# Late rms factor in the fronts, another order in the attention to the memory, and C and D normalised on ScalarE

## The chip, the cores and the metric

The kernel runs on one core of a Trainium2 chip. A core has TensorE (PE in the profile), VectorE (DVE), ScalarE (ACT), GpSimd (POOL) and SyncE (SP), which issues the transfers. Each engine takes its instructions in the order in which the built program lists them and waits at an instruction until its semaphores allow it. The metric is the device time of one execution in microseconds, lower is better.

## The reference

Two layers of an encoder over 512 tokens of width 1024, in float32, with 256 memory tokens. A layer has three residual sub-layers: a mixer with four parallel attention branches A, B, C and D, each projected, gated and summed; an attention to the memory with four heads; and a squared-ReLU MLP. Every softmax attention scales its queries and keys by an rms norm per head, and that is what the change touches:

```
def rms(x, g):
    y = xf * lax.rsqrt(jnp.mean(xf * xf, axis=-1, keepdims=True) + EPS)
    return (y * g.astype(F32)).astype(x.dtype)
...
q = axial_rope(rms(q, g_qk[0]), row, col)
k = axial_rope(rms(k, g_qk[1]), row, col)
sc = jnp.einsum('bqgrd,bkgd->bgrqk', qg, k).astype(F32) * scale
p = jax.nn.softmax(sc, axis=-1)
```

The rms factor is one number per token and head. The gain works per channel, and the rotation mixes two channels of the same head, so the factor may be multiplied in before or after both.

## The kernel before

Matrix products run in a split form: an operand is a high part (rounded to the matmul's float32r) and a low part (the remainder), and `mm3` (L176) issues three matmuls, high by high, high by low and low by high, at L177 to L179. Weights come from DRAM into `wst` (3 buffers), ACT casts them to `whi` (L299, 4 buffers) and POOL subtracts to get `wlo` (L167 with POOL, four pieces for each tile).

The mixer of a layer is a list of units: four of B (a pair of heads each), four of A (one head), two of C and two of D (a group of four heads). A unit has a *front* and an *attention*. A front projects four blocks of 128 tokens (`tok_proj`, L386), evacuates each block from PSUM to `tok` and sums the squares per head into `sf` (`evac_sq`, L406 to L416), and then works in halves of two blocks each (`half`): the rms factor by `rpow` (L309: POOL adds, then POOL raises to the power -0.5), the factor times q and k on DVE (L452 in A, L552 in C and D, L722 in B), the gain (L454, L555, L557, L725), the rotation in B and D (`rope`, L576, at L584 to L587), the split into `spl` (ACT casts the high part, DVE subtracts for the low part, shown at L167 with DVE), and PE transposes of `spl` (`trans`, L399, shown at L403 in PE). The attention of a unit runs over 128 queries at a time: scores into an `sc` bank, maximum on DVE, exponentials on ACT with their sum (L634 in C, L638 in D), reciprocal of the sum (L640) and the product with it on DVE (L641), transposes on PE (L476), the split of the transposed `pt` (L479 on ACT, L480 on DVE), and the product with v.

Between the units stand pieces of the gates and branch projections, given by the string `FILL` (L90), chained in order of issue, so that PE has work while a front or an attention waits. The order of the whole program on each engine is set when it is built, by a scheduler that works from the order of issue, the buffers and its own estimate of durations.

The attention to the memory (`xattn`, L899) projects the queries of all four blocks first (`proj`, L907; PSUM tag `dn` with 2 banks), norms and splits each block (`xnorm_split`, L884), transposes them (`q_trans`, L910), and attends for two pairs of blocks and two pairs of heads (`attend`, L917), then projects out (L962). PSUM has 2 banks for `dn`, 2 for `sc`, 2 for `tr`, 1 for `pv` and 1 for `df`.

Of the kernel before, what the change touches and what calls it, by code (L numbers as in the profile page):

```python
# [93 lines left out]
def kernel(  # L94
# [41 lines left out]
    def ptile():  # L136
        return tl("p", [P, S + 2])
# [4 lines left out]
    def stat(n):  # L142
        return tl("st", [P, 8])[:, :n]
# [287 lines left out]
    def front_A(l, norm, h):  # L431
# [15 lines left out]
        def half(j):  # L447
# [85 lines left out]
    def front_G(l, norm, br, g):  # L533
# [14 lines left out]
        def half(j):  # L548
            tk, s = toks[j], st[j]
            rpow(s, s, 64 * EPS, 10)  # L550
            qk = tk[:, :, :320].rearrange("p t (h d) -> p t h d", h=5)
            V.tensor_tensor(out=qk, in0=qk, in1=bc(s.rearrange("p (t h) -> p t h", t=2), 3, 64), op=ALU.mult)  # L552
# [23 lines left out]
    def rope(x, tab, j, nh, nax):  # L576
# [3 lines left out]
        tmp = tl("zr", [P, S])[:, :2 * nh * w].rearrange("p (t h d) -> p t h d", t=2, h=nh)  # L580
# [22 lines left out]
    def attn_G(l, u, br, g, oslots):  # L603
# [5 lines left out]
        for j in range(4):  # L609
# [6 lines left out]
            for pr in range(2):  # L616
# [3 lines left out]
                for qi in range(2):  # L620
# [20 lines left out]
                    V.tensor_scalar(e, e, st[:, 2:3], None, op0=ALU.mult)  # L641
# [50 lines left out]
    def front_B(l, cT, p):  # L692
# [20 lines left out]
        for j in range(2):  # L713
            tk, s = toks[j]
            s3 = s.rearrange("p (t c) -> p t c", t=2)
            G.tensor_scalar(s3[:, :, 0:4], s3[:, :, 0:4], 64 * EPS, None, op0=ALU.add)
            G.tensor_scalar(s3[:, :, 4:6], s3[:, :, 4:6], 32 * EPS, None, op0=ALU.add)
            G.tensor_tensor(out=s, in0=s, in1=mhalf[:, :12], op=ALU.pow)
# [3 lines left out]
            V.tensor_tensor(out=qk, in0=qk, in1=bc(s3[:, :, 0:4], 3, 64), op=ALU.mult)  # L722
            V.tensor_tensor(out=qr, in0=qr, in1=bc(s3[:, :, 4:6], 3, 32), op=ALU.mult)
# [4 lines left out]
            rope(qr, bt_, j, 2, 1)  # L728
            sq_ = tl("spl", [P, 2, 2, 2, 96], F32R)
# [90 lines left out]
    def mem_prep(l):  # L820
# [3 lines left out]
        for c in range(2):  # L824
            st = tl("wst", [P, 4, NM])
            SY.dma_start(st, memT[c * 512:(c + 1) * 512, :].rearrange("(k p) t -> p k t", p=P))
            for k in range(4):
# [8 lines left out]
                else:  # L836
                    q = tl("zr", [P, S])[:, :NM]
# [61 lines left out]
    def xattn(l, norm, KT, VX, X, nm):  # L899
# [7 lines left out]
        def proj(pr):  # L907
            tok_proj(norm, views, S, ev, tbs=(2 * pr, 2 * pr + 1))
# [8 lines left out]
        def attend(pr):  # L917
            for hp in range(2):
                if hp == 1 and pr == 0:
                    q_trans(1)  # L920
                pth = tl("pt", [P, 2, 2, 256], F32R)
                ptl = tl("pt", [P, 2, 2, 256], F32R)
                for qi in range(2):
                    Tq = Tqs[2 * pr + qi]
                    ps = psum("sc").rearrange("p (h k) -> p h k", h=2)
                    for i in range(2):
                        h = 2 * hp + i
                        hs = slice(h * P, (h + 1) * P)
                        mm3(ps[:, i], Tq[:, 0, hs], Tq[:, 1, hs], KT[0][:, h, :], KT[1][:, h, :], True, True)
                    st = stat(6)  # L930
                    V.tensor_reduce(out=st[:, 0:2], in_=ps, axis=AX.X, op=ALU.max, negate=True)
                    e = ptile()[:, :S].rearrange("p (h k) -> p h k", h=2)
                    for i in range(2):
                        A.activation(e[:, i], ps[:, i], AF.Exp, bias=st[:, i:i + 1], accum_out=st[:, 2 + i:3 + i])
                    V.reciprocal(st[:, 4:6], st[:, 2:4])
                    V.tensor_tensor(out=e, in0=e, in1=bc(st[:, 4:6], 2, NM), op=ALU.mult)
                    qs = slice(qi * P, qi * P + P)
                    pt = psum("tr")
                    for i in range(2):
                        for kb in range(2):  # L940
                            T.transpose(pt[:, (2 * i + kb) * P:(2 * i + kb + 1) * P], e[:, i, kb * P:(kb + 1) * P], idf)
                    pv_ = pt.rearrange("p (k q) -> p k q", k=4)
                    hi = pth[:, :, :, qs].rearrange("p h k q -> p (h k) q")
                    lo = ptl[:, :, :, qs].rearrange("p h k q -> p (h k) q")
                    A.copy(hi, pv_)
                    V.tensor_tensor(out=lo, in0=pv_, in1=f(hi), op=ALU.subtract)
                po = psum("pv").rearrange("p (h q) -> p h q", h=2)
                for i in range(2):
                    h = 2 * hp + i
                    for kb in range(2):  # L950
                        hs = slice(h * P, (h + 1) * P)
                        mm3(po[:, i], VX[0][:, kb, hs], VX[1][:, kb, hs], pth[:, i, kb, :], ptl[:, i, kb, :], kb == 0,
                            kb == 1)
                for i in range(2):
# [321 lines left out]
```

## Time and profile before

| | |
|---|---|
| median of 3 runs | 2363.65 us (2363.37 to 2367.36) |
| profiled execution | 2361.96 us |
| its span, first to last instruction | 2360.0 us |
| PE busy | 2281.5 us, 97% of the span |
| DVE, ACT, POOL busy | 1384.1, 1151.8, 1299.0 us |
| mean granted PE clock | 0.992 of full speed |
| chain that ended last | PE 83%, DVE 11%, POOL 2% |

A time on the device holds the span and about 2 us around it. PE's busy time is the time in which at least one matmul is under way; matmuls overlap each other, so that two of them start 0.23 us apart while each is shown with 0.39 us. An idle stretch of PE is printed in brackets behind the instruction that ended it, with the instruction that released it. The granted clock is 1.00 at 2.4 GHz and 0.50 at 1.2 GHz. The layers lie at 20 to 1206 us and 1206 to 2360 us; in the first, B takes about 20 to 225 us, A to 430, C to 537, D to 690, the last branch work and the output projection to 764, the attention to the memory to 850, and the MLP the rest.

### The profile page before, as it was taken

What the parts mean: (1) busy time and instruction counts of PE and PEld (TensorE: products, weight loads), DVE (VectorE), ACT (ScalarE), POOL (GpSimd) and SP (SyncE); (2) the same over time, 40 slices, a digit from 0 to 9 for tenths busy, and PEclk for the clock granted to TensorE, in tenths of its full rate; (3) what the DMA queues carried; (4) which work ended last, traced back from release to release, by engine and by line L of the source; (5) the groups of instructions that cost most, each with busy time, mean ns of one, the idle gap of its engine ahead of it and who ended that gap; (6) DMA issues with size and microseconds to landing.
All of it is one profiled execution on the core that took longest, in us unless ns stands there. A gap on an engine that the chain in (4) does not pass through costs nothing.

```text
span 2360.0 us, 33643 instructions
## 1 busy us (share of the span) xinstructions
PE 2281.5 (97%) x12032; PEld 1966.0 (83%) x12032; DVE 1384.1 (59%) x2980; ACT 1151.8 (49%) x2253; POOL 1299.0 (55%) x1657
## 2 busy tenths in 40 slices
PE   8999999998999899999999998999989999999999
PEld 7888889887888888888888887898878878888887
DVE  7778666888975642222457786568879648222222
ACT  4556556655653543223345565566556546322321
POOL 7553544625465376666665435355353754766663
PEclk9999999999999999999999999999999999999999
DMA  5321342442454133333343214324425531323332
GB/s 185 108 94 57 102 138 66 127 154 84 147 179 155 54 99 98 98 92 96 111 134 101 83 46 127 113 79 134 136 92 168 171 131 56 106 91 97 98 93 77
DMA packets 88775, 258.25 MB, mean 109 GB/s; under 512 B 9704, under 2 KB 12392, under 8 KB 88608
## 3 DMA queue, kind: packets, MB, share of 16 engines
q1 hardware_dynamic: 88608, 256.10, 34.4%
q8 instruction: 95, 1.56, 0.3%
q14 instruction: 72, 0.59, 0.1%
HBM read 222.46 MB, written 33.60 MB: 109 GB/s over the span
## 4 chain that ended last, share of the span: by engine, by line
PE 83%; DVE 11%; POOL 2%; issue 1%; ACT 1%; DMA 1%; SPq 0%; POOLq 0%; ACTq 0%; DVEq 0%
PE dn L177 13%; PE dn L178 13%; PE dn L179 13%; PE df L177 10%; PE df L179 9%; PE df L178 9%; PE tr L476 3%; PE sc L177 1%; PE sc L179 1%; PE sc L178 1%; PE dn L403 1%; POOL wlo L167 1%; DVE pt L480 1%; DVE zr L584 1%; PE sc L624 1%
## 5 line engine op out<-in xcount | busy, mean ns | idle before, releaser
L167 POOL TENSOR_TENSOR wlo<-wst,whi 128x256 fp32r<-128x256 f32 (+3 forms) x1400 | 1071.0, 797 | 745.4 <-ACT whi L299 671.3
L299 ACT CAST whi<-wst 128x1024 fp32r<-128x1024 f32 (+3 forms) x350 | 348.8, 1003 | 640.8 <-PE dn L178 293.7
L177 PE MATMUL df<-s,whi 128*128 128x512 f32 (+1 forms) x967 | 381.0, 394 | 8.1 <-DVE zg L785 3.2
L179 PE MATMUL df<-s,wlo 128*128 128x512 f32 (+1 forms) x967 | 376.1, 389 | 1.3 <-POOL wlo L167 1.3
L178 PE MATMUL df<-s,whi 128*128 128x512 f32 (+1 forms) x967 | 374.3, 387 | 1.6 <-DVE s L167 1.6
L177 PE MATMUL dn<-whi,s 128*128 128x384 f32 (+4 forms) x768 | 264.8, 348 | 13.6 <-ACT s L348 7.7
L179 PE MATMUL dn<-whi,s 128*128 128x384 f32 (+4 forms) x768 | 263.3, 343 | 0.0
L178 PE MATMUL dn<-wlo,s 128*128 128x384 f32 (+4 forms) x768 | 263.1, 344 | 0.0
L177 PEld LDWEIGHTS df<-s,whi 128*128 128x128 f32 x967 | 181.7, 188 | 46.6 <-DVE yl L808 6.1
L179 PEld LDWEIGHTS df<-s,wlo 128*128 128x128 f32 x967 | 181.8, 188 | 38.4 <-POOL wlo L167 2.9
L178 PEld LDWEIGHTS df<-s,whi 128*128 128x128 f32 x967 | 181.9, 188 | 34.3 <-DVE s L167 2.2
L178 PE MATMUL dn<-s,whi 128*128 128x512 f32 (+1 forms) x529 | 197.1, 373 | 0.0
L179 PE MATMUL dn<-s,wlo 128*128 128x512 f32 (+1 forms) x529 | 196.9, 373 | 0.0
L177 PE MATMUL dn<-s,whi 128*128 128x512 f32 (+1 forms) x529 | 196.5, 374 | 0.0
L177 PEld LDWEIGHTS dn<-whi,s 128*128 128x128 f32 x768 | 146.8, 192 | 24.5 <-ACT s L348 7.7
L480 DVE TENSOR_TENSOR pt<-tr,pt 128x512 fp32r<-128x512 f32 (+1 forms) x224 | 142.7, 644 | 26.0 <-ACT pt L479 17.3
L178 PEld LDWEIGHTS dn<-wlo,s 128*128 128x128 f32 x768 | 147.2, 192 | 8.9 <-POOL wlo L167 0.2
L179 PEld LDWEIGHTS dn<-whi,s 128*128 128x128 f32 x768 | 146.8, 191 | 6.9
L479 ACT CAST pt<-tr 128x512 fp32r<-128x512 f32 (+1 forms) x224 | 121.8, 556 | 55.9 <-PE tr L476 54.3
L311 POOL TENSOR_SCALAR sf<-sf 128x8 f32<-128x8 f32 (+2 forms) x44 | 13.9, 316 | 241.3 <-DVE sf L415 239.5
L179 PEld LDWEIGHTS dn<-s,wlo 128*128 128x128 f32 x529 | 99.6, 188 | 17.9 <-POOL wlo L167 0.2
L178 PEld LDWEIGHTS dn<-s,whi 128*128 128x128 f32 x529 | 99.6, 188 | 17.8
(376 smaller groups left out, 4827.3 us busy)
## 6 DMA issues: line engine op xcount, KB each, us to landing
wst<-in_wts_dram SPq DMA_DIRECT2D x272, 512.0 KB, 3.5
wst<-in_wts_dram SPq DMA_DIRECT2D x64, 384.0 KB, 3.1
yl<-yz SPq DMA_DIRECT2D x48, 512.0 KB, 4.0
yz<-zg SPq DMA_DIRECT2D x64, 256.0 KB, 2.2
yz<-yl SPq DMA_DIRECT2D x48, 256.0 KB, 3.0
bias<-tscr SPq DMA_DIRECT2D x16, 320.0 KB, 3.3
yl<-yz SPq DMA_DIRECT2D x16, 256.0 KB, 3.1
bias<-tscr SPq DMA_DIRECT2D x8, 448.0 KB, 3.5
```

The costliest lines, as they stand in the source:

```text
L167: (eng or V).tensor_tensor(out=dst, in0=src, in1=f(hi), op=ALU.subtract)
L177: a = T.matmul(ps, lhsT=lh, rhs=rh, start=first, stop=False)
L178: T.matmul(ps, lhsT=lh, rhs=rl, start=False, stop=False)
L179: b = T.matmul(ps, lhsT=ll, rhs=rh, start=False, stop=last)
L299: chain("wh", A.copy(hi[:, :n], st[:, :n]))
L311: G.tensor_scalar(dst, src, add, None, op0=ALU.add)
L403: T.transpose(ps[:rows_, i * P:(i + 1) * P], s, idn)
L476: T.transpose(ps[:, kb * P:(kb + 1) * P], src[:, kb * P:(kb + 1) * P], idn)
L479: A.copy(hi, pv)
L480: V.tensor_tensor(out=lo, in0=pv, in1=f(hi), op=ALU.subtract)
L584: V.tensor_tensor(out=tmp[:, :, :, o:o + 16], in0=x[:, :, :, oo:oo + 16], in1=bc(tab[:, 1, b2, o:o + 16], 2, nh), op=ALU.mult)
L624: T.matmul(ps[:, :nk], lhsT=q, rhs=Tk[:, 0, kb0 * P:kb0 * P + nk], start=True, stop=False)
```

## The change

There are three parts. The rms factor comes late: the sum plus epsilon moves from POOL to DVE, the power stays on POOL but is issued at high priority, and DVE multiplies the factor into q and k after the gain and, in B and D, after the rotation. In D the rotation of q and of k becomes one of five heads. Second, the attention to the memory is issued as projection of blocks 0 and 1, transposes, attention, block 2, attention, block 3, transposes, attention, and blocks 2 and 3 use the single `df` bank. Third, in C and D the exponentials times the reciprocal sums run on ACT.

```
     def rpow(dst, src, add, n):
-        G.tensor_scalar(dst, src, add, None, op0=ALU.add)
-        G.tensor_tensor(out=dst, in0=dst, in1=mhalf[:, :n], op=ALU.pow)
+        V.tensor_scalar(dst, src, add, None, op0=ALU.add)
+        with tc.high_priority():
+            G.tensor_tensor(out=dst, in0=dst, in1=mhalf[:, :n], op=ALU.pow)
...
-            V.tensor_tensor(out=qk, in0=qk, in1=bc(s.rearrange("p (t h) -> p t h", t=2), 3, 64), op=ALU.mult)
             for m in range(2):
                 V.tensor_tensor(out=kk[:, :, m], in0=kk[:, :, m], in1=bc(ga, 1, 2), op=ALU.mult)
+            V.tensor_tensor(out=qk, in0=qk, in1=bc(s.rearrange("p (t h) -> p t h", t=2), 3, 64), op=ALU.mult)
...
             else:
                 V.tensor_tensor(out=qk, in0=qk, in1=bc(gd, 1, 2), op=ALU.mult)
-                rope(qk[:, :, 0:4], dt_, j, 4, 2)
-                rope(qk[:, :, 4:5], dt_, j, 1, 2)
+                rope(qk, dt_, j, 5, 2)
+            rpow(s, s, 64 * EPS, 10)
+            V.tensor_tensor(out=qk, in0=qk, in1=bc(s.rearrange("p (t h) -> p t h", t=2), 3, 64), op=ALU.mult)
...
                     V.reciprocal(st[:, 2:3], st[:, 1:2])
-                    V.tensor_scalar(e, e, st[:, 2:3], None, op0=ALU.mult)
+                    A.activation(e, e, AF.Copy, scale=st[:, 2:3])
...
-        def proj(pr):
-            tok_proj(norm, views, S, ev, tbs=(2 * pr, 2 * pr + 1))
+        def proj(*tbs):
+            tok_proj(norm, views, S, ev, tbs=tbs, tags=("dn", "dn", "df", "df"))
...
-        proj(0)
-        proj(1)
+        proj(0, 1)
         q_trans(0)
-        attend(0)
-        attend(1)
+        attend(0, 0)
+        proj(2)
+        attend(0, 1)
+        proj(3)
+        q_trans(1)
+        attend(1, 0)
+        attend(1, 1)
```

The first place is POOL in the second unit of A, around the rms factor `sf_3256` of its second half. Before:

```order
L167 TENSOR_TENSOR wlo_3357<-wst_3354,whi_3356 128x256 x4
L167 TENSOR_TENSOR wlo_3567<-wst_3564,whi_3566 128x192 x4
L167 TENSOR_TENSOR wlo_3576<-wst_3573,whi_3575 128x192 x4
L311 TENSOR_SCALAR sf_3256<-sf_3256 128x8
L167 TENSOR_TENSOR wlo_3585<-wst_3582,whi_3584 128x192 x4
L312 TENSOR_TENSOR sf_3256<-sf_3256,mhalf 128x8
L167 TENSOR_TENSOR wlo_3594<-wst_3591,whi_3593 128x192 x4
```

And now, on the same engine at the same place:

```order
L167 TENSOR_TENSOR wlo_3357<-wst_3354,whi_3356 128x256 x4
L167 TENSOR_TENSOR wlo_3567<-wst_3564,whi_3566 128x192 x4
L167 TENSOR_TENSOR wlo_3576<-wst_3573,whi_3575 128x192 x4
L313 TENSOR_TENSOR sf_3256<-sf_3256,mhalf 128x8
L167 TENSOR_TENSOR wlo_3585<-wst_3582,whi_3584 128x192 x4
L167 TENSOR_TENSOR wlo_3594<-wst_3591,whi_3593 128x192 x4
```

The addition is gone from POOL, and the power stands ahead of the four pieces of `wlo_3585`. The twelve pieces ahead of it stay.

The second place is DVE in the first unit of D, second half (`tok_6115`), up to the split of q. Before:

```order
L552 TENSOR_TENSOR tok_6115<-tok_6115,sf_6116 128x640
L557 TENSOR_TENSOR tok_6115<-tok_6115,gd 128x640
L584 TENSOR_TENSOR zr_6198<-tok_6115,ropd_t 128x8x16 x4
L586 TENSOR_TENSOR tok_6115<-tok_6115,ropd_t 128x2x256
L587 TENSOR_TENSOR tok_6115<-tok_6115,zr_6198 128x2x256
L785 TENSOR_TENSOR zg_6308<-df_6283,Rrow 128x512
L584 TENSOR_TENSOR zr_6205<-tok_6115,ropd_t 128x2x16 x4
L595 TENSOR_TENSOR of_5812<-pv_5901,z_5982 64x512
L167 TENSOR_TENSOR spl_6212<-tok_6115,spl_6212 128x8x64
```

And now, the last twelve rows up to the late factor (the gain and the four products of the rotation stand up to 11 rows further up):

```order
L586 TENSOR_TENSOR tok_6115<-tok_6115,ropd_t 128x640
L640 RECIPROCAL st_5948<-st_5948 128x1
L786 TENSOR_TENSOR zg_6256<-df_6231,Rrow 128x512
L174 COPY T_6026<-dn_6175 128x2x256
L630 ISA p_5947,st_5948<-sc_5944,bias_5899,nsink 128x384
L630 ISA st_5948 128x1
L633 COPY p_5947<-nsink 128x1
L167 TENSOR_TENSOR s_5809<-of_5636,s_5809 128x512
L587 TENSOR_TENSOR tok_6115<-tok_6115,zr_6188 128x640
L481 TENSOR_TENSOR pt_5857<-tr_5868,pt_5856 128x3x128
L481 TENSOR_TENSOR pt_5857<-tr_5884,pt_5856 128x3x128
L559 TENSOR_TENSOR tok_6115<-tok_6115,sf_6116 128x640
```

The factor, which headed the sequence, now ends it, and work of the attention of C stands between its steps.

The third place is ACT in the attention to the memory of the first layer, from the first evacuation of the queries. Before:

```order
L412 ACTIVATE tok_8497<-dn_8472,r_x 128x512
L413 ACTIVATE dn_8472<-dn_8472,r_x 128x512
L412 ACTIVATE tok_8533<-dn_8508,r_x 128x512
L413 ACTIVATE dn_8508<-dn_8508,r_x 128x512
L895 CAST spl_8505<-tok_8497 128x512
L895 CAST spl_8541<-tok_8533 128x512
L412 ACTIVATE tok_8569<-dn_8544,r_x 128x512
```

And now:

```order
L413 ACTIVATE tok_8469<-dn_8444,r_x 128x512
L414 ACTIVATE dn_8444<-dn_8444,r_x 128x512
L413 ACTIVATE tok_8505<-dn_8480,r_x 128x512
L414 ACTIVATE dn_8480<-dn_8480,r_x 128x512
L413 ACTIVATE tok_8628<-df_8603,r_x 128x512
L414 ACTIVATE df_8603<-df_8603,r_x 128x512
L896 CAST spl_8477<-tok_8469 128x512
L896 CAST spl_8513<-tok_8505 128x512
```

The split of blocks 0 and 1 now stands behind the evacuation of block 2 (`df_8603`). On PE the transposes of `spl_8477` follow the last matmul of `df_8603`, and the projection of block 3 (`df_8700`) follows them.

## Rows read from the trace of the kernel before

**Rows 1.** The head of the page and its line of busy times.

```profile
span 2360.0 us, 33643 instructions
PE 2281.5 (97%) x12032; PEld 1966.0 (83%) x12032; DVE 1384.1 (59%) x2980; ACT 1151.8 (49%) x2253; POOL 1299.0 (55%) x1657
```

**Rows 2.** Busy time by stretch: the stretch, its length, then busy microseconds (and instructions) of PE, PEld, DVE, ACT and POOL, the granted clock, DMA share and GB/s. The stretches are A and D of the first layer.

```profile
225.00:430.00 205.00, 197.05 (x1148) 179.18 (x1146) 132.38 (x317) 119.89 (x260) 103.07 (x148) 0.98 0.32 100
...
537.00:690.00 153.00, 144.30 (x797) 125.38 (x798) 128.67 (x252) 92.33 (x186) 82.17 (x100) 0.97 0.41 129
```

**Rows 3.** The same view, same columns, of six stretches in which the granted clock is at half; the last row sums all six, and the two left out lie in the attention to the memory.

```profile
296.40:303.20 6.80, 4.63 (x20) 4.31 (x21) 5.36 (x14) 2.28 (x6) 2.72 (x5) 0.50 0.64 218
549.00:559.20 10.20, 7.04 (x28) 6.82 (x29) 5.17 (x13) 2.48 (x5) 0.70 (x2) 0.50 0.27 83
...
1470.60:1477.40 6.80, 5.88 (x24) 5.56 (x25) 4.12 (x12) 1.81 (x4) 1.55 (x2) 0.50 0.41 133
1723.20:1730.00 6.80, 5.48 (x24) 5.26 (x24) 3.39 (x8) 0.90 (x2) 0.00 (x0) 0.50 0.24 77
...
sum 37.40, PE 29.52 PEld 28.44 DVE 23.26 ACT 11.10 POOL 11.43; mean PE 4.92 PEld 4.74 DVE 3.88 ACT 1.85 POOL 1.91
```

**Rows 4.** PE in order of time, only rows that begin after an idle stretch: start, time, instruction, and in brackets the idle time and its releaser. The first four are in A and D, the others in the attention to the memory.

```profile
298.20 0.72 PE L403 MATMUL dn<-jr,spl 128*128 128x128 f32 x4 [3.83 <-DVE spl L167]
...
551.65 0.59 PE L403 MATMUL dn<-idr,spl 128*128 128x128 f32 x3 [5.42 <-DVE spl L167]
...
1471.15 0.72 PE L403 MATMUL dn<-jr,spl 128*128 128x128 f32 x4 [3.81 <-DVE spl L167]
...
1724.02 1.23 PE L403 MATMUL dn<-idr,spl 128*128 128x128 f32 x8 [3.88 <-DVE spl L167]
...
773.39 0.50 PE L177 MATMUL dn<-whi,s 128*128 128x512 f32 x1 [1.60 <-DVE sf L415]
...
791.61 0.58 PE L177 MATMUL sc<-T,T 128*128 128x256 f32 x1 [3.12 <-ACT p L934]
...
1958.60 0.52 PE L177 MATMUL sc<-T,T 128*128 128x256 f32 x1 [2.93 <-ACT p L934]
```

**Rows 5.** The chain in A that ends in the wait at 298.20 us, by engine in order of time (same columns): POOL, then DVE.

```profile
283.28 7.28 POOL L167 TENSOR_TENSOR wlo<-wst,whi 128x256 fp32r<-128x256 f32 x12 [5.84 <-ACT whi L299]
...
290.97 2.28 POOL L167 TENSOR_TENSOR wlo<-wst,whi 128x192 fp32r<-128x192 f32 x4
293.20 1.67 POOL L312 TENSOR_TENSOR sf<-sf,mhalf 128x8 f32<-128x8 f32 x1
...
287.40 0.42 DVE L415 TENSOR_REDUCE sf<-dn 128x4 f32<-128x256 f32 x1 [0.51 <-ACT dn L413]
...
295.07 0.90 DVE L452 TENSOR_TENSOR tok<-tok,sf 128x512 f32<-128x512 f32 x1
...
297.64 1.08 DVE L167 TENSOR_TENSOR spl<-tok,spl 128x256 fp32r<-128x256 f32 x3
```

**Rows 6.** The chain in D that ends in the wait at 551.65 us, in the same way.

```profile
538.46 2.28 POOL L167 TENSOR_TENSOR wlo<-wst,whi 128x192 fp32r<-128x192 f32 x4
540.71 1.98 POOL L312 TENSOR_TENSOR sf<-sf,mhalf 128x10 f32<-128x10 f32 x1
...
537.29 0.47 DVE L415 TENSOR_REDUCE sf<-dn 128x5 f32<-128x320 f32 x1
...
542.72 1.22 DVE L552 TENSOR_TENSOR tok<-tok,sf 128x640 f32<-128x640 f32 x1 [1.81 <-POOL sf L312]
543.97 1.11 DVE L557 TENSOR_TENSOR tok<-tok,gd 128x640 f32<-128x640 f32 x1
545.11 1.59 DVE L584 TENSOR_TENSOR zr<-tok,ropd_t 128x128 f32<-128x128 f32 x4
...
549.22 0.84 DVE L584 TENSOR_TENSOR zr<-tok,ropd_t 128x32 f32<-128x32 f32 x4
```

**Rows 7.** ACT in the attention to the memory, in order of time: the first evacuation of the queries and the second split.

```profile
771.37 0.69 ACT L412 ACTIVATE tok<-dn,r_x 128x512 f32<-128x512 f32 x1 [6.94 <-PE dn L179]
...
777.52 0.62 ACT L895 CAST spl<-tok 128x512 fp32r<-128x512 f32 x1 [1.31 <-DVE tok L891]
```

**Rows 8.** Groups of instructions by line and shape over the whole span (count, then busy microseconds, mean nanoseconds of one, and idle time before them).

```profile
L641 DVE TENSOR_SCALAR p<-p,st 128x512 f32<-128x512 f32 x64 | 38.1, 598 | 0.8
L641 DVE TENSOR_SCALAR p<-p,st 128x384 f32<-128x384 f32 x64 | 29.1, 470 | 1.0
...
L634 ACT ACTIVATE p<-p,st 128x385 f32<-128x385 f32 x64 | 39.7, 622 | 32.7 <-DVE p L633 16.3 <-DVE st L630 15.9
...
L412 ACT ACTIVATE tok<-dn,r_x 128x512 f32<-128x512 f32 x8 | 5.5, 688 | 15.9 <-PE dn L179 15.9
```

**Rows 9.** Who waited for whom (microseconds in total, times, longest): ACT in C and D of the first layer and of the second, PE in C and D of the first layer, PE in A of the first layer, PE in B of the first layer.

```profile
ACT v L424 <- PE dn L179: 17.8, 6, 7.4
...
ACT v L424 <- PE dn L179: 16.9, 6, 6.6
...
PE pv L647 <- ACT p L634: 0.9, 1, 0.9
...
PE dn L403 <- DVE spl L167: 4.7, 2, 3.8
...
PE dn L403 <- ACT spl L732: 1.1, 1, 1.1
```

More of the change, by code (lines that the diff above doesn't have):

```diff
@@ L715, in front_B @@
             s3 = s.rearrange("p (t c) -> p t c", t=2)
-            G.tensor_scalar(s3[:, :, 0:4], s3[:, :, 0:4], 64 * EPS, None, op0=ALU.add)
-            G.tensor_scalar(s3[:, :, 4:6], s3[:, :, 4:6], 32 * EPS, None, op0=ALU.add)
-            G.tensor_tensor(out=s, in0=s, in1=mhalf[:, :12], op=ALU.pow)
+            V.tensor_scalar(s3[:, :, 0:4], s3[:, :, 0:4], 64 * EPS, None, op0=ALU.add)
+            V.tensor_scalar(s3[:, :, 4:6], s3[:, :, 4:6], 32 * EPS, None, op0=ALU.add)
+            with tc.high_priority():
+                G.tensor_tensor(out=s, in0=s, in1=mhalf[:, :12], op=ALU.pow)
             qr = tk[:, :, 0:64].rearrange("p t (h d) -> p t h d", h=2)
@@ L728, in front_B @@
             rope(qr, bt_, j, 2, 1)
+            V.tensor_tensor(out=qk, in0=qk, in1=bc(s3[:, :, 0:4], 3, 64), op=ALU.mult)
+            V.tensor_tensor(out=qr, in0=qr, in1=bc(s3[:, :, 4:6], 3, 32), op=ALU.mult)
             sq_ = tl("spl", [P, 2, 2, 2, 96], F32R)
@@ L836, in mem_prep @@
                 else:
-                    q = tl("zr", [P, S])[:, :NM]
+                    q = tl("zr", [P, 640])[:, :NM]
                     A.activation(q, st[:, k, :], AF.Square)
@@ L915, in q_trans @@
                 Tqs.append(Tq)
[L917 to L947, printed above, removed]
@@ L948, in attend @@
+        def attend(pr, hp):
+            pth = tl("pt", [P, 2, 2, 256], F32R)
+            ptl = tl("pt", [P, 2, 2, 256], F32R)
+            for qi in range(2):
+                Tq = Tqs[2 * pr + qi]
+                ps = psum("sc").rearrange("p (h k) -> p h k", h=2)
                 for i in range(2):
                     h = 2 * hp + i
-                    for kb in range(2):
-                        hs = slice(h * P, (h + 1) * P)
-                        mm3(po[:, i], VX[0][:, kb, hs], VX[1][:, kb, hs], pth[:, i, kb, :], ptl[:, i, kb, :], kb == 0,
-                            kb == 1)
@@ L954, in attend @@
-                for i in range(2):
-                    h = 2 * hp + i
-                    ds_ = slice(pr * 256, pr * 256 + 256)
-                    A.copy(xo[h][:, 0, ds_], po[:, i])
-                    V.tensor_tensor(out=xo[h][:, 1, ds_], in0=po[:, i], in1=f(xo[h][:, 0, ds_]), op=ALU.subtract)
+                    hs = slice(h * P, (h + 1) * P)
+                    mm3(ps[:, i], Tq[:, 0, hs], Tq[:, 1, hs], KT[0][:, h, :], KT[1][:, h, :], True, True)
+                st = stat(6)
+                V.tensor_reduce(out=st[:, 0:2], in_=ps, axis=AX.X, op=ALU.max, negate=True)
@@ new lines, in attend @@
+                e = ptile()[:, :S].rearrange("p (h k) -> p h k", h=2)
+                for i in range(2):
+                    A.activation(e[:, i], ps[:, i], AF.Exp, bias=st[:, i:i + 1], accum_out=st[:, 2 + i:3 + i])
+                V.reciprocal(st[:, 4:6], st[:, 2:4])
+                V.tensor_tensor(out=e, in0=e, in1=bc(st[:, 4:6], 2, NM), op=ALU.mult)
+                qs = slice(qi * P, qi * P + P)
+                pt = psum("tr")
+                for i in range(2):
+                    for kb in range(2):
+                        T.transpose(pt[:, (2 * i + kb) * P:(2 * i + kb + 1) * P], e[:, i, kb * P:(kb + 1) * P], idf)
@@ new lines, in attend @@
+                pv_ = pt.rearrange("p (k q) -> p k q", k=4)
+                hi = pth[:, :, :, qs].rearrange("p h k q -> p (h k) q")
+                lo = ptl[:, :, :, qs].rearrange("p h k q -> p (h k) q")
+                A.copy(hi, pv_)
+                V.tensor_tensor(out=lo, in0=pv_, in1=f(hi), op=ALU.subtract)
+            po = psum("pv").rearrange("p (h q) -> p h q", h=2)
+            for i in range(2):
+                h = 2 * hp + i
+                for kb in range(2):
+                    hs = slice(h * P, (h + 1) * P)
+                    mm3(po[:, i], VX[0][:, kb, hs], VX[1][:, kb, hs], pth[:, i, kb, :], ptl[:, i, kb, :], kb == 0,
+                        kb == 1)
@@ L960, in xattn @@
+            for i in range(2):
+                h = 2 * hp + i
+                ds_ = slice(pr * 256, pr * 256 + 256)
+                A.copy(xo[h][:, 0, ds_], po[:, i])
+                V.tensor_tensor(out=xo[h][:, 1, ds_], in0=po[:, i], in1=f(xo[h][:, 0, ds_]), op=ALU.subtract)
         w = []
```

6 lines of the change are left out of this document (1 added, 5 removed).

## The prediction

> **What bounds the kernel now.** I read the busy times first. PE is busy for 2281.5 of 2360.0 us [rows 1], so only two things can change the time: the 78 us in which PE stands still, and the time it works at the half clock. The change leaves every matmul in place.
>
> Next I read PE in order of time, for idle stretches only [rows 4]. Two waits of 3.83 and 3.81 us stand in A, and two of 5.42 and 3.88 us in D, all ended by DVE's split of q and k. Three waits of 1.60, 3.12 and 2.93 us stand in the attention to the memory. Behind each of these but the one of 1.60 us, the granted clock is 0.50, the 1.2 GHz level, for some microseconds [rows 3]; behind that one it did not fall. In the half-clock stretches PE is busy for 29.52 us, of which half is lost: in A (4.63 + 5.88) / 2 = 5.25 us, in D (7.04 + 5.48) / 2 = 6.26, and in the attention to the memory the rest, (29.52 - 23.03) / 2 = 3.2. So a wait that is shortened enough pays twice.
>
> Then I followed the two chains back. In A [rows 5] the last statistic is there at 287.40 + 0.42 = 287.82 us. POOL is inside twelve pieces of weights until 290.56, does the addition, then four more pieces until 293.25, and only then the power, which ends at 294.87. The factor starts at 295.07, and PE, free at 298.20 - 3.83 = 294.37, starts at 298.20. In D [rows 6] the statistic is there at 537.76; the power waits behind four pieces and ends at 542.69. DVE stands idle for the last 1.81 us before the factor, then gain, rotation and split follow it.
>
> **A, late factor.** The order puts the power right behind the twelve pieces and the four behind it. By the same durations: 290.56 + 1.67 (power) + 0.2 (gap to DVE as before) + 0.90 (factor) = 293.33. From the end of the factor to PE's start it took 298.20 - 295.97 = 2.23 us, gain included. With all of it PE starts at 295.56 and waits 1.2 us; with the gain gone ahead, as the order has it, it might wait some tenths. The other end is the old wait, if the estimate of the order fails because POOL reaches the twelve pieces later. I take 1.2, since the casts of the split share ACT with casts of weights. Two waits: (3.83 - 1.2) + (3.81 - 1.2) = 5.2 us. At 1.2 us, below the 1.60 that brought no fall, the half clock goes too: 5.25. PE's waits for this split total 4.7 us in the first layer, so 0.9 lies in the smaller one [rows 9]; half of it in each layer is 0.9. **A: -11.4** (bounds -16 and 0).
>
> The four pieces that now follow the power come 1.67 us later by the power itself and earlier by the addition; the next weights could be late by that. The addition on DVE is a 128x8 instruction, beside reductions of 0.42 us; it lies in DVE's idle time.
>
> **D, late factor and rotation of five heads.** The wait for POOL (1.81 us) is filled with the rotation. The gain (1.11 us) is issued before the last statistic and leaves the chain. The products of one head, four for 0.84 us, go into the four of the others, 1.59 us [rows 6], which grow from 128x128 to 128x160: about 0.6 saved. Together 3.5 of 5.42, leaving 1.9. If foreign rows fill the place of the saved work, as the order at this place allows, only the 1.81 counts and 3.6 is left; if the foreign rows fall outside, the wait could vanish. I take 1.9 and, in the second layer in the same proportion, 3.88 x 1.9 / 5.42 = 1.4. Gain 3.5 + 2.5 = 6.0, and the half clock, 6.26, since both lie nearer to 1.60 than to 2.93. **D: -12.3** (bounds -16 and +2, the latter if DVE's order costs a wait more).
>
> **B.** It gets the same edit, but PE waits there for the split only once, 1.1 us [rows 9], so nothing large can be won. The scheduler moved the transposes there too. The open direction is up: a wait like A's, 3.8 plus 2.6 of clock, in each layer would be +12.8. I take a little: **+1.9**, half of one such wait.
>
> **C and D, the product on ACT.** 64 instructions of 598 ns and 64 of 470 ns, 67.2 us, leave DVE [rows 8]. On ACT the nearest rows are 688 ns at 128x512 (scaled evacuation) and 622 ns at 128x385 (exponential): 64 x 0.688 + 64 x 0.622 = 83.8 us, or 16.6 more than on DVE. ACT has the room: in D of a layer it is busy for 92.33 of 153 us against DVE's 128.67 [rows 2], and 32 products make that 114.3 against 109.6. The price is in the chain of one block of queries: exponential on ACT, reciprocal on DVE, then back to ACT's queue, ahead of PE's transposes. If every one of 128 paid its extra duration it would be 16.6 us; PE's wait for p is 0.9 us in a layer now [rows 9]. Below, DVE's relief could shorten what remains in D, at most its 1.9 + 1.4 = 3.3. I take the row of PE's wait, doubled in both layers: **+1.8** (bounds -3.3 and +16.6).
>
> The Trainium skill (ScalarE: Activation LUTs, "Rules for kernel authors") says that a multiplication belongs on VectorE and not on ScalarE, because VectorE is the faster by element. The trace agrees on the price (598 against 688 ns), and by the rule this part alone would cost up to the 16.6 us above; the busy times in D speak for the move nevertheless.
>
> **The attention to the memory.** Block 2 is projected before the transposes of block 0, so the wait of 1.60 for its bank goes. But ACT evacuates block 2 before it casts the split of block 0 (the third place of the order). PE would be through with block 2's 24 matmuls (eight blocks of the width, three each) at 773.39 - 1.60 + 24 x 0.23 = 777.3 us; then follow its evacuation (0.69, and as much for the squares), the cast (0.62) [rows 7] and DVE's half of the split (about as long): PE starts near 780.0 and waits 2.7 in the place of 1.60. In return projection of blocks 2 and 3 now lies beside the exponentials, where PE waited 3.12 and 2.93. I count 2 x (2.7 - 1.6) = +2.2, half of 3.12 + 2.93 gone = -3.0, and a third of the clock's 3.2 = -1.1. **-2** (bounds: all those waits and the clock gone, 2 x 1.60 + 6.05 + 3.2 = -12.5; the new waits stand beside the old ones with a half clock of their own, 2 x 2.7, and 2 x 2.5, half of the mean of the six stretches, 4.92 [rows 3], = +10.4).
>
> **Sum.** -11.4 - 12.3 + 1.9 + 1.8 - 2 = -22.0. On the profiled execution's own time, 2361.96 (its span and 1.96 around it), that gives 2340.0. The median of the runs is 1.69 above the profiled one, so 2341.7, rounded to **2342**.
>
> **The rivals.** First, DVE becomes the bound of D. For it: DVE is busy there for 84% of the stretch, and in the order work of C's attention stands between the steps of the rotation. Against it: DVE gives 19 us of L641 away there. Then D keeps its waits and half clock, and A's -11.4 remains with the small terms, +1.7: 2363.65 - 9.7 = about 2354.
>
> Second, the waits only move. For it: each chain ends in a transpose whose cover the scheduler chose by its own estimates, and where a chain gets shorter it may put the transposes as much earlier, leaving PE as late as before. Against it: in A the twelve pieces and the matmuls before the transposes stand where they stood. Then 2362, no change.
>
> Third, slower: ACT's queue. ACT takes its instructions in order, and in C and D it stands for 17.8 us (six times) in one layer and 16.9 us (six times) in the other at the evacuation of v, waiting for PE [rows 9], 2.9 us a time. A product that stands behind such an instruction holds up PE's transposes, which were free of it on DVE. If all twelve reach PE it is +34.7, with the gains 2363.65 - 22.0 + 34.7 = about 2376; from eight of the twelve on the change is a loss. Against it: PE usually has projections between exponentials and transposes.
>
> **How the numbers follow.** The forecast has 0.58, with a likely range of its own from 2333 to 2351. D bound by DVE has 0.16, the waits that move 0.12, ACT's queue 0.14. A measurement tells a change from none at about 0.2%, 4.7 us, so faster means below 2358.9: the forecast and the first rival, 0.74. Same: 0.12. Slower: 0.14. The range goes from 2329, with the larger gains of A, D and the memory attention partly together, to 2365, which takes in the first two rivals and leaves most of the third out.
>
> **What the profile after would show.** Right in A: the power directly behind the twelve pieces, waits near 1.2 us at both places, and no stretch at 0.50 behind them. Right in D: no idle time of DVE before the factor, waits below 2 us, and a full clock. In the attention to the memory a new wait of PE for the split at the first transposes, near 2.7 us. For C and D, ACT as the releaser of PE's transposes for little more than a microsecond in each layer. Wrong would be: waits of 3 us or more in D on the split (first rival), the same idle total of 78 us under other lines (second), or PE's transposes released by ACT with ACT waiting on PE before (third).

## The result and the profile after

The changed kernel takes 2327.6 us (median of 4, 2326.4 to 2330.3) against 2365.5 us beside it (median of 4): ratio 0.9841, 95% interval 0.9824 to 0.9858. It is faster, as forecast, but the time lies 1.4 us below the low end of the range (2329), and the gain is 37.9 us where 22 were worked out. The head of the page after, which answers to [rows 1]:

```profile
span 2325.5 us, 33553 instructions
PE 2270.2 (98%) x12032; PEld 1958.4 (84%) x12032; DVE 1337.9 (58%) x2888; ACT 1213.4 (52%) x2381; POOL 1271.9 (55%) x1573
```

PE's share of the chain that ended last rose from 83 to 87%, and DVE's fell from 11 to 7%:

```profile
PE 87%; DVE 7%; issue 2%; POOL 1%; DMA 1%; ACT 1%; SPq 0%; DVEq 0%; ACTq 0%; POOLq 0%
```

The span is 34.5 us shorter with the same 12032 matmuls. PE's idle time fell from 78.5 to 55.3 us, and its busy time by 11.3, most of it half-clock time that is gone. The stages C and D of the first layer after, by the columns of [rows 2]:

```profile
422.00:526.30 104.30, 102.00 (x605) 93.58 (x604) 80.87 (x237) 79.07 (x180) 49.03 (x60) 1.00 0.48 147
526.30:670.40 144.10, 141.85 (x801) 124.30 (x800) 105.73 (x206) 112.54 (x222) 69.73 (x90) 0.99 0.41 133
```

D took 153 us before, with PE idle for 8.7 of them; now 144.1, idle for 2.2. DVE and ACT are about evenly busy there, as forecast (109.6 and 114.3). PE in order of time after idle stretches, as in [rows 4], in A, D and the attention to the memory:

```profile
292.01 0.51 PE L404 MATMUL dn<-jr,spl 128*128 128x128 f32 x4 [1.00 <-DVE spl L167]
...
549.86 0.39 PE L647 MATMUL pv<-pt,v 128*128 128x256 f32 x1 [1.28 <-ACT pt L480]
550.62 0.44 PE L177 MATMUL dn<-whi,s 128*128 128x384 f32 x1 [0.38 <-DVE sf L416]
...
757.28 0.54 PE L404 MATMUL tr<-idr,spl 128*128 128x128 f32 x4 [1.86 <-ACT spl L896]
767.23 0.39 PE L177 MATMUL sc<-T,T 128*128 128x256 f32 x1 [0.91 <-ACT p L932]
...
1703.97 0.38 PE L647 MATMUL pv<-pt,v 128*128 128x256 f32 x1 [1.29 <-ACT pt L480]
```

A's 3.83 is 1.00, and both waits of D for the split are gone. In the second layer's A the wait for the split is gone too. The chain of A after, POOL and DVE, which answers to [rows 5]:

```profile
279.93 7.38 POOL L167 TENSOR_TENSOR wlo<-wst,whi 128x256 fp32r<-128x256 f32 x12 [5.59 <-ACT whi L299]
287.27 1.63 POOL L313 TENSOR_TENSOR sf<-sf,mhalf 128x8 f32<-128x8 f32 x1
288.88 4.91 POOL L167 TENSOR_TENSOR wlo<-wst,whi 128x192 fp32r<-128x192 f32 x7
```

```profile
284.56 0.41 DVE L416 TENSOR_REDUCE sf<-dn 128x4 f32<-128x256 f32 x1
285.00 0.17 DVE L311 TENSOR_SCALAR sf<-sf 128x8 f32<-128x8 f32 x1
...
288.94 1.08 DVE L455 TENSOR_TENSOR tok<-tok,sf 128x512 f32<-128x512 f32 x1 [1.09 <-POOL sf L313]
...
291.18 2.16 DVE L167 TENSOR_TENSOR spl<-tok,spl 128x256 fp32r<-128x256 f32 x3 [0.39 <-ACT spl L458]
```

The power begins the moment the twelve pieces end, and the factor follows it. The half clock after (same columns as [rows 3]; the four stretches lie in D and in the attention to the memory, none in A; the last microseconds of either kernel, at half too, are left out):

```profile
551.56:554.97 3.41, 3.41 (x13) 3.41 (x12) 2.41 (x8) 2.46 (x6) 0.23 (x1) 0.50 0.00 0
773.42:776.83 3.41, 3.41 (x17) 3.41 (x18) 3.08 (x5) 0.47 (x2) 2.11 (x2) 0.50 0.11 30
1705.26:1708.67 3.41, 3.41 (x13) 3.41 (x12) 2.65 (x11) 2.88 (x7) 0.00 (x0) 0.50 0.00 0
1927.13:1930.54 3.41, 3.41 (x19) 3.36 (x18) 2.89 (x5) 0.82 (x2) 1.92 (x2) 0.50 0.15 12
```

PE is busy in them for 13.64 us where it was for 29.52: 7.9 us less lost.

To see where time goes by stage, two traces are laid beside each other at equal work: each matmul counts with the median distance between starts of its shape, and a stage ends where this sum is what it was before at the times of the stages. Changes against the profile of before, both layers together, in us (D with the branch work behind it):

| kernel | B | A | C | D | memory | span |
|---|---|---|---|---|---|---|
| forecast | +1.9 | -11.4 | the product: +1.8 | -12.3 | -2 | -22.0 |
| changed | -3.1 | -11.5 | -3.5 | -17.5 | +0.6 | -34.5 |
| late_alone | -2.4 | -11.3 | +1.3 | -10.4 | +2.9 | -19.7 |
| act_alone | +1.6 | +1.4 | +0.8 | -9.4 | -0.2 | -5.7 |
| mem_alone | +1.0 | +4.5 | +1.4 | -1.6 | +0.9 | +6.1 |
| act_left_out | -2.9 | -11.3 | +1.3 | -9.8 | +2.6 | -19.3 |
| mem_left_out | -2.2 | -11.6 | -3.9 | -20.3 | +1.3 | -37.2 |

A stage is certain to some 2 us, at times worse: the +4.5 of mem_alone stands in a stage whose code it does not touch. The times of several runs decide; the table says where to look.

### The profile page after: what moved, and what is told of

It reads as the page before. It is cut to its first block, busy times and chain, and to the rows that moved or that the text cites. A ratio compares the mean times of both kernels' runs of the same rounds, so it can differ in the third digit from the quotient of the medians.

```text
span 2325.5 us, 33553 instructions
## 1 busy us (share of the span) xinstructions
PE 2270.2 (98%) x12032; PEld 1958.4 (84%) x12032; DVE 1337.9 (58%) x2888; ACT 1213.4 (52%) x2381; POOL 1271.9 (55%) x1573
## 4 chain that ended last, share of the span: by engine, by line
PE 87%; DVE 7%; issue 2%; POOL 1%; DMA 1%; ACT 1%; SPq 0%; DVEq 0%; ACTq 0%; POOLq 0%
PE dn L177 13%; PE dn L178 13%; PE dn L179 13%; PE df L177 11%; PE df L178 10%; PE df L179 10%; PE tr L477 3%; PE dn L404 1%; PE sc L177 1%; PE sc L179 1%; PE sc L178 1%; PE pv L647 1%; PE sc L624 1%; PE sc L625 1%; PE pv L648 1%
## 5 line engine op out<-in xcount | busy, mean ns | idle before, releaser
L177 PE MATMUL dn<-whi,s 128*128 128x384 f32 (+4 forms) x736 | 250.1, 345 | 9.1 <-ACT s L349 7.6
L179 PE MATMUL dn<-whi,s 128*128 128x384 f32 (+4 forms) x736 | 251.1, 341 | 0.0
L178 PE MATMUL dn<-wlo,s 128*128 128x384 f32 (+4 forms) x736 | 250.8, 341 | 0.0
L313 POOL TENSOR_TENSOR sf<-sf,mhalf 128x8 f32<-128x8 f32 (+2 forms) x44 | 73.8, 1677 | 223.8 <-DVE sf L311 172.7
L481 DVE TENSOR_TENSOR pt<-tr,pt 128x512 fp32r<-128x512 f32 (+1 forms) x224 | 143.1, 644 | 33.8 <-ACT pt L480 16.7
L177 PEld LDWEIGHTS dn<-whi,s 128*128 128x128 f32 x736 | 139.6, 190 | 18.5 <-ACT s L349 7.6
L480 ACT CAST pt<-tr 128x512 fp32r<-128x512 f32 (+1 forms) x224 | 122.1, 555 | 49.4 <-PE tr L477 48.2
L178 PEld LDWEIGHTS dn<-wlo,s 128*128 128x128 f32 x736 | 140.0, 190 | 7.6
L179 PEld LDWEIGHTS dn<-whi,s 128*128 128x128 f32 x736 | 139.7, 190 | 5.6
```

Source lines behind the costliest of these rows:

```text
L177: a = T.matmul(ps, lhsT=lh, rhs=rh, start=first, stop=False)
L178: T.matmul(ps, lhsT=lh, rhs=rl, start=False, stop=False)
L179: b = T.matmul(ps, lhsT=ll, rhs=rh, start=False, stop=last)
L480: A.copy(hi, pv)
L481: V.tensor_tensor(out=lo, in0=pv, in1=f(hi), op=ALU.subtract)
```

## The experiments

### The three parts, alone and left out

The theory after the result is that the late factor carries nearly all of the gain (theory 1 below); its rivals are that the product on ACT carries what lies beyond the forecast (theory 2), and that DVE bounds D without it (theory 3). Each kernel takes one or two of the three parts of the diff: the late factor (`rpow` and the fronts), the order in `xattn`, and L641. Expected of late_alone:

> The kernel before with the first part alone: late rms factor in A, B, C and D, the addition on DVE, the power at high priority, the rotation of five heads in D. Theory 1 (the late factor carries nearly all): A -11.5, B -3, D -15, C -3, so about 2332 us, and the waits of 5.42 and 3.88 in D below 2. Theory 2 (the prediction's sizes for the late factor, and the product on ScalarE carries what lies beyond them): A -11.4 and D -12 at most, nothing in B and C, about 2341. Theory 3 (DVE is the bound of D without the product moved): only A gains, about 2354, with waits of 3 us or more left in D.

Of act_alone:

> The kernel before with the product of the exponentials on ScalarE alone. Theory 1: within 3 us of before, about 2365 (+1.8 as in the prediction). Theory 2: the relief of DVE gains by itself in C and D, 8 us or more: 2357 or less, with D's waits of 5.42 and 3.88 shortened by a microsecond or two. Rival of the prediction (the queue of ScalarE): slower, 2372 or more.

Of late_left_out:

> The changed kernel without the late factor (attention to the memory in the new order, product on ScalarE). Theory 1: within 3 us of before, about 2365. Theory 2: about 2357. If the product helps only where the late factor is there, this one and the product alone give nothing, and the product left out costs more than the product alone gains.

Of act_left_out:

> The changed kernel with the product back on VectorE. Theory 1: within 3 us of the changed kernel, about 2329. Theory 2: it loses 8 us or more, 2336 to 2341, and the loss lies in C and D. Theory 3: D gets its waits of 3 us or more back, about 2350.

Of mem_alone:

> The kernel before with the new order of the attention to the memory alone. From the changed kernel's profile (0.3 us less in one layer, 0.9 more in the other): within 2 us of before, about 2365. By the prediction: -2, about 2363. If the waits ahead of that stage changed its alignment, up to 5 either way.

Of mem_left_out:

> The changed kernel with the old order of the attention to the memory: late factor and product alone. If the order is worth nothing: within 2 us of the changed kernel, about 2327. By the prediction: +2, about 2330.

Measured, with the ratio to the kernel before on the same chip:

| run | median us | ratio and interval |
|---|---|---|
| late_alone | 2342.2 | 0.9894 (0.9878 to 0.9911) |
| act_alone | 2355.4 | 0.9946 (0.9927 to 0.9965) |
| late_left_out | 2357.6 | 0.9961 (0.9948 to 0.9974) |
| act_left_out | 2341.6 | 0.9892 (0.9877 to 0.9908) |
| mem_alone | 2365.8 | 1.0004 (0.9993 to 1.0014) |
| mem_left_out | 2325.9 | 0.9833 (0.9815 to 0.9851) |

Theory 2 holds. The runs stand beside different runs of the kernel before, so the ratios are compared. The product on ACT is worth 12 us alone (2367.4 beside it) and 0.9892 - 0.9841 = 0.0051, again 12 us, in the changed kernel; the first part, late factor and joint rotation, 25 alone and 0.9961 - 0.9841 = 0.0120, 28 us, in the changed kernel. The order in the attention to the memory is worth nothing that stands out of the noise. The parts add up: 0.9894 x 0.9946 = 0.9841.

What PE waits for in C and D of the first layer tells how they fit together (columns as in [rows 9]). First the kernel before (its L480 is L481 in the others), then late_alone, then the changed kernel:

```profile
PE tr L476 <- DVE pt L480: 0.5, 1, 0.5
...
PE pv L648 <- DVE pt L480: 0.2, 1, 0.2
```

```profile
PE pv L648 <- DVE pt L481: 3.1, 3, 1.4
PE tr L477 <- DVE pt L481: 2.9, 2, 2.1
PE pv L647 <- ACT p L634: 0.9, 1, 0.9
```

```profile
PE pv L647 <- ACT pt L480: 1.3, 1, 1.3
PE df L177 <- DVE yl L809: 1.1, 1, 1.1
PE pv L647 <- DVE of L595: 0.7, 1, 0.7
...
PE tr L477 <- DVE pt L481: 0.3, 1, 0.3
...
PE pv L648 <- DVE pt L481: 0.2, 1, 0.2
```

With the late factor alone the front's wait of 5.42 us is gone, but 3.1 + 2.9 = 6.0 us stand in the attention, where 0.7 stood before and where PE waits for the low half of the transposed probabilities, work of DVE. With the product away from DVE, 0.5 of that is left. Without the late factor the relief works on the front's own wait: in act_alone 5.42 us became 3.6, and 3.88 in the second layer 3.0:

```profile
PE dn L403 <- DVE spl L167: 3.6, 1, 3.6
...
PE dn L403 <- DVE spl L167: 3.0, 1, 3.0
```

### Relief of DVE, or the shorter chain?

Three edits of the changed kernel at L641, in this order: product_left_out, vector_load_back (`dump` is a tile of zeros), act_product_twice.

```
-                    A.activation(e, e, AF.Copy, scale=st[:, 2:3])
...
+                    V.tensor_scalar(dump[:, :nk], dump[:, :nk], st[:, 2:3], None, op0=ALU.mult)
                     A.activation(e, e, AF.Copy, scale=st[:, 2:3])
...
                     A.activation(e, e, AF.Copy, scale=st[:, 2:3])
+                    A.activation(e, e, AF.Copy, scale=1.0)
```

> The changed kernel with the product of the exponentials and the reciprocal sums left out of C and D altogether (the probabilities stay unnormalised there). If the gain of the move is the relief of VectorE alone and ScalarE hides the product: within 3 us of the changed kernel, 2324 to 2330. If the product on ScalarE costs something in the chain from the exponentials to the transposes: well below, 2320 or less.

> The changed kernel with an extra product of the same size on VectorE behind each reciprocal, into a tile of zeros that nothing reads: VectorE gets its 67 us back, the product that is used stays on ScalarE. If the relief of VectorE makes the gain: it is lost, about 2341, as with the product back on VectorE. If the gain lies in the shorter chain or in another order instead: it stays, about 2328.

> The changed kernel with a second pass of ScalarE over each block of exponentials in C and D (times 1.0), 128 instructions more. If ScalarE has the room and the chain has cover: at most 2 us slower, 2330 or less. If the chain carries it: 128 x 0.65 us is 83 us more at most, and each twentieth of it that PE sees is 4 us, so 2332 or more.

Measured: 2331.6 (0.9859, 0.9845 to 0.9874), 2340.5 (0.9899, 0.9883 to 0.9915) and 2336.0 us (0.9877, 0.9856 to 0.9898). Without any product the kernel is not faster than with it on ACT; it came out 4 us slower by the ratio, which the intervals do not tell apart, and 1.6 us above the expected range. So ACT hides the product, unless the new order of that run cost as much as the product would have given. With the load back on DVE, in a tile that nobody reads, the gain is gone (ratio 0.9899 against 0.9892 with the product itself back), and PE again waits for DVE in C and D of the first layer, though not for the same instructions as in late_alone (`of` holds the output of the attention, `yl` a gated branch projection; the edit moves L481 to L483):

```profile
PE pv L650 <- DVE of L597: 2.0, 2, 1.7
PE df L177 <- DVE yl L812: 1.8, 1, 1.8
...
PE pv L651 <- DVE pt L483: 0.9, 2, 0.7
PE tr L479 <- DVE pt L483: 0.9, 1, 0.9
```

So it is DVE's time in its queue that PE paid for. One run would not show it, since each edit also gives a new order, and one (rope_in_two, below) moved the time by as much; but the product put on ACT alone, taken off ACT again, and its load put back on DVE give the same 12 to 14 us. ACT is not free without end: a second pass, 73 us of ACT, costs 8.4 us, so the second reading of its expectation holds.

### What in the late factor makes the gain

Edits of the changed kernel: `rpow` as before everywhere (power_as_before), or in C and D alone (power_old_in_cd); the addition on DVE but the power without priority (no_priority); the factor back ahead of gain and rotation, with the early power kept (early_factor); D's rotation in two parts (rope_in_two). In this order power_as_before, no_priority, early_factor (A; in the other fronts likewise) and rope_in_two; in B the sum and the power are edited as in `rpow`, and power_old_in_cd writes the two lines of the first edit into `half` of C and D:

```
-        V.tensor_scalar(dst, src, add, None, op0=ALU.add)
-        with tc.high_priority():
-            G.tensor_tensor(out=dst, in0=dst, in1=mhalf[:, :n], op=ALU.pow)
+        G.tensor_scalar(dst, src, add, None, op0=ALU.add)
+        G.tensor_tensor(out=dst, in0=dst, in1=mhalf[:, :n], op=ALU.pow)
...
-        with tc.high_priority():
-            G.tensor_tensor(out=dst, in0=dst, in1=mhalf[:, :n], op=ALU.pow)
+        G.tensor_tensor(out=dst, in0=dst, in1=mhalf[:, :n], op=ALU.pow)
...
+            V.tensor_tensor(out=qk, in0=qk, in1=bc(s.rearrange("p (t h) -> p t h", t=2), 3, 64), op=ALU.mult)
             for m in range(2):
                 V.tensor_tensor(out=kk[:, :, m], in0=kk[:, :, m], in1=bc(ga, 1, 2), op=ALU.mult)
-            V.tensor_tensor(out=qk, in0=qk, in1=bc(s.rearrange("p (t h) -> p t h", t=2), 3, 64), op=ALU.mult)
...
-                rope(qk, dt_, j, 5, 2)
+                rope(qk[:, :, 0:4], dt_, j, 4, 2)
+                rope(qk[:, :, 4:5], dt_, j, 1, 2)
```

> The changed kernel with addition and power both on GpSimd and without the high priority, as before; the factor stays late. If the late place of the factor makes the gain in A and D: about 2328 to 2332. If the earlier power makes it: A has its waits of 3.8 us back, about 2340 to 2350.

> The changed kernel with the factor multiplied in ahead of gain and rotation again in A, B, C and D, but with the addition on VectorE and the power at high priority. If the early power alone makes A's gain: A stays as in the changed kernel (within 1 us), and D loses what the late place brings, up to 6 us a layer, so 2332 to 2340. If A needs the late factor as well: A loses 3 us or more a layer, 2340 or more.

> The changed kernel without the high priority of the power; the addition stays on VectorE, the factor late. If the priority brings the power forward: A gets back the 6 us a layer of power_as_before, about 2337. If it is enough that the addition has left GpSimd: A stays, about 2328.

> The changed kernel with addition and power on GpSimd and without the high priority in C and D alone; A and B keep the new form. From the stages of the run with the old power everywhere (D 2.9 and 3.6 us shorter than in the changed kernel, A 6.2 and 6.2 longer): about 6 us less, 2321, faster than the changed kernel. If those 6 us were an accident of that run's order: 2326 to 2330.

> The changed kernel with D's rotation in two parts again, four heads and one. The prediction put 0.6 us on the joint one in each of four chains: 2.4 us in all if all of it reaches the end, so 2328 to 2330; nothing if VectorE has the slack now.

| run | median us | ratio and interval | A, both layers, against the changed kernel |
|---|---|---|---|
| power_as_before | 2337.0 | 0.9879 (0.9864 to 0.9894) | +12.3 |
| early_factor | 2364.7 | 0.9990 (0.9978 to 1.0003) | +21.1 |
| no_priority | 2328.0 | 0.9838 (0.9824 to 0.9852) | -0.1 |
| power_old_in_cd | 2327.9 | 0.9844 (0.9829 to 0.9858) | +0.4 |
| rope_in_two | 2343.0 | 0.9909 (0.9894 to 0.9924) | -0.3 |

In A both halves are needed. With the old power the late factor leaves a wait of 3.15 us, and all of A's gain is lost (the 2337.0 lies below the 2340 of the second reading because D came out shorter in that run):

```profile
295.53 0.72 PE L403 MATMUL dn<-jr,spl 128*128 128x128 f32 x4 [3.15 <-DVE spl L167]
```

The priority does nothing: it is enough that the addition has left POOL. In no_priority the power still stands directly behind the twelve pieces (the view starts among them) and ahead of the next weights:

```profile
284.39 2.87 POOL L167 TENSOR_TENSOR wlo<-wst,whi 128x192 fp32r<-128x192 f32 x5
287.23 1.63 POOL L312 TENSOR_TENSOR sf<-sf,mhalf 128x8 f32<-128x8 f32 x1
288.83 5.46 POOL L167 TENSOR_TENSOR wlo<-wst,whi 128x192 fp32r<-128x192 f32 x8
```

In C and D the early power is worth nothing, and the 6 us that power_as_before seemed to win there did not come again in power_old_in_cd. The early factor with the early power loses the whole gain (ratio 0.9990): the second reading of its expectation holds, and by far more than it said. Its trace in A, POOL and then DVE (same columns as [rows 5]):

```profile
291.00 1.64 POOL L313 TENSOR_TENSOR sf<-sf,mhalf 128x8 f32<-128x8 f32 x1
292.60 5.02 POOL L167 TENSOR_TENSOR wlo<-wst,whi 128x192 fp32r<-128x192 f32 x8
```

```profile
292.67 2.75 DVE L453 TENSOR_TENSOR tok<-tok,sf 128x512 f32<-128x512 f32 x1 [0.98 <-POOL sf L313]
...
295.94 1.22 DVE L455 TENSOR_TENSOR tok<-tok,ga 128x128 f32<-128x128 f32 x2
```

The factor is there early, but takes 2.75 us where it took 0.90 before, and the gain still follows it. PE waits 3.2 us behind it. So what is won by the power is lost at the factor and the gain. A loses 21.1 us in both layers in the profile, and the stages beside it lose about as much. Most of it is the clock: fifteen stretches stand at half (columns as in [rows 3]), and PE is busy in them for 74.17 us, against 13.64 in the changed kernel. Half of the difference is 30 of the 42.1 us by which this span is the longer one; the profiled execution is the slowest of ten (2354.9 to 2369.4).

```profile
sum 81.80, PE 74.17 PEld 67.56 DVE 49.28 ACT 29.18 POOL 9.91; mean PE 4.94 PEld 4.50 DVE 3.29 ACT 1.95 POOL 0.66
```

rope_in_two cost 15 us where 2.4 at most were expected. DVE is busy for only 0.6 us more in each of the eight rotations, by the groups of both traces. The trace puts 9.5 us into D and the work behind it, where a wait of 2.0 us for DVE appears in the second layer, and 5.0 into the attention to the memory, whose waits are nearly the same and whose half clock is 10.24 us long at 774 us in place of 3.41, with one more stretch of 3.41 us in each layer. The place is shown, the cause of the size is not; the edit gave DVE a new order. So how much of D's gain belongs to the late factor and how much to the joint rotation stays open.

### Can it be carried further?

power_old_in_cd_b_act replaces the same line of `attn_B` as the change does in `attn_G`, on top of power_old_in_cd; old_mem_old_cd_power puts together the old attention to the memory and the old power in C and D, and changed_again is the changed kernel beside it.

> The run power_old_in_cd, and in B the product of the exponentials with the reciprocal sums on ScalarE too: 64 instructions of 128x512 leave VectorE, which is busy for 155 of 203 us in B of the first layer, with ScalarE busy for 112. If relief of VectorE pays in B as in C and D: 3 to 6 us less than power_old_in_cd. If PE does not wait for VectorE there: within 2 us of it.

> The changed kernel once more, beside the next one: 2326 to 2330.

> The changed kernel with the old order of the attention to the memory and with the old power in C and D (GpSimd, no priority); A, B, the late factor and the product on ScalarE as in the changed kernel. From the stages: the old order of the attention to the memory went with 1.5 us less in D of each layer, the old power with 2 us less in C and D of the first: 2322 to 2325 if these add up, 2326 to 2330 if they were accidents of the order.

Measured: 2331.1 (2324.8 to 2335.9), 2329.2 and 2327.4 us; ratios 0.9856 (0.9837 to 0.9874), 0.9843 (0.9829 to 0.9857) and 0.9835 (0.9821 to 0.9849). None is told apart from the changed kernel. In B the move did not pay: the median is 3.2 us above power_old_in_cd, outside both readings, but its runs spread over 11 us. PE's largest wait for DVE in B of the first layer, for the gates' `zg`, is 2.4 us without the move and 2.7 with it.

## Why the prediction was right or wrong

**Right: A, its clock in part by luck.** Forecast -11.4, found -11.5 in the profile (-11.3 in late_alone and act_left_out), with the wait at 1.00 us (1.2 forecast) in the first layer, none in the second, and no half clock. The rows of before held two terms. The power does come right behind the twelve pieces. From the end of the factor to PE's start it is 1.99 us in place of 2.23: the gain has gone ahead, but the cast of the split stands behind a cast of weights on ACT, as the forecast had allowed for:

```profile
290.00 0.84 ACT L299 CAST whi<-wst 128x768 fp32r<-128x768 f32 x1 [2.29 <-PE df L178]
290.74 0.40 ACT L458 CAST spl<-tok 128x256 fp32r<-128x256 f32 x1
```

The third term, that below 1.60 us the half clock goes, was luck in part. changed_again, a second profile of the same kernel, has the wait at 1.05 us, the same 0.68 us as here (293.70 us) behind it, and then a stretch at half (columns as in [rows 3]), half of it or 1.7 us lost:

```profile
292.18 0.52 PE L404 MATMUL dn<-jr,spl 128*128 128x128 f32 x4 [1.05 <-DVE spl L167]
```

```profile
294.64:298.05 3.41, 3.41 (x12) 3.31 (x11) 2.29 (x7) 0.82 (x2) 1.01 (x1) 0.50 0.67 238
```

The runs add that it takes both edits, which the sum had put in one line: it reached the 1.2 us with the gain still behind the factor, and early_factor, which has it there, waits 3.2. They also show that the moved addition alone brings the power forward.

**Right in kind: D's late factor.** Both waits for the split are gone, where 1.9 and 1.4 were forecast. But late_alone shows -10.4 in D and behind it, not more, since 6.0 us of waits for DVE came up in the attention of the first layer. That is the first rival, DVE as the bound of D, with 0.16: by the late factor alone it would have come true in part, with the waits in the attention and not, as it said, at the split. The 0.6 us for the joint rotation is DVE's saving in rope_in_two as well, but that run lost 15 us, so what the rotation gives in D is not settled.

**Wrong: the product on ACT.** The failed step is "I take the row of PE's wait, doubled in both layers: +1.8 (bounds -3.3 and +16.6)". The measured value is -12 to -14 (act_alone, act_left_out and vector_load_back), far below the lower bound. The duration was right (83.3 us on ACT, 83.8 forecast):

```profile
L641 ACT ACTIVATE p<-p,st 128x512 f32<-128x512 f32 x64 | 44.6, 727 | 1.5 <-DVE st L640 1.5
...
L641 ACT ACTIVATE p<-p,st 128x384 f32<-128x384 f32 x64 | 38.7, 614 | 4.9 <-DVE st L640 4.6
```

The lower bound was the mistake. It counted what the late factor would leave of D's two front waits, 3.3 us, as all that DVE's relief could win. But DVE at 84% of D [rows 2] is a queue in which everything behind is late by it, and once the front no longer waits, the next wait on the same queue is what PE sees. Bounded by DVE's load it would have read: of the 67.2 us taken off DVE some part between nothing and all. The runs give a fifth of it. The price that the step did count is not seen: PE's wait for p [rows 9] is not among the changed kernel's waits in C and D. The Trainium skill (ScalarE: Activation LUTs, "Rules for kernel authors") sends multiplications to VectorE as the faster by element; in float32 here it is the faster (598 against 727 ns over 128x512), and the move pays all the same, because PE waited for VectorE's queue and not for ScalarE's.

**Wrong, small: the others.** B came out at -3.1 and not +1.9: no new wait for the split came, and the one of 1.1 us in the first layer is 0.7. The attention to the memory at +0.6 and not -2, with mem_alone at no change: the new wait of 1.86 us (2.7 forecast) is there in each layer, the 3.12 went to 0.91, and four waits of 0.5 to 0.9 between scores and products took up what that gave.

**The rivals.** ACT's queue did not decide: ACT waits at the evacuation of v for only 4.9 us in C and D of a layer, against 17.8 and 16.9 [rows 9]. That waits only move is true of the attention to the memory, and in part of D with the late factor alone.

Of the 12.5 us between 22.0 and 34.5 in the profile the product makes more than all (12 to 14 gained where 1.8 were to be lost); the other misses nearly cancel. The 3.4 us between 34.5 and 37.9 come from the profiled execution of before, 2361.96, which lay 3.6 us below the median of the runs beside the result.

## What to carry to other kernels

Before a price is put on work that is moved from one engine to another, add up all waits of the bounding engine that the relieved engine ends, the ones behind the present longest too: when the longest goes, the next on the same queue appears, and two edits on one queue are to be judged together. A chain that runs over a slow helper engine is shortened by having everything ready that can be ready before its result, and by taking the helper's other small steps away; either alone gave nothing in A.

## What had not been expected of the hardware

A product on DVE with two inputs in SBUF can be held up by POOL. The factor of A over 128x512 took 0.68 us where POOL stood still and up to 1.17 beside its pieces of weights in the changed kernel, and in early_factor, where it began 0.07 us behind the first of a run of pieces, 2.75 us, and 3.46 at 335.56 us. In the first of these POOL's first four pieces kept their 0.60 us each, and the fifth, during which the factor ended, took 1.04. The Trainium skill (GPSIMD Engine Reference, "Specifications") says that the SBUF interfaces are shared with VectorE and that instructions with two SBUF inputs contend; the trace agrees, and shows that the loser can stand for four pieces. What lets it through sooner is not shown: in the changed kernel the factor at 288.94 us began 0.06 us behind the first piece too, and took 1.08.

The half clock came behind waits of 1.28 and 0.38 us in a row (549.86 and 550.62), each shorter than the 1.60 us of [rows 4] behind which it had not come. Nor does the length of one wait settle it. Behind a wait of 1.86 us at the transposes of the attention to the memory in the second layer, the granted clock fell in no_priority, where these rows stand (columns as in [rows 4] and [rows 3]), and in the changed kernel it stayed at 1.00:

```profile
1910.69 0.68 PE L403 MATMUL tr<-idr,spl 128*128 128x128 f32 x4 [1.86 <-ACT spl L894]
```

```profile
1910.84:1914.25 3.41, 3.41 (x11) 2.78 (x11) 2.31 (x5) 1.05 (x2) 1.38 (x1) 0.50 0.00 0
```

A term for the half clock is therefore safer as a range than as one value.
